# Attention rows split later in attention and earlier in the projection, kept among the sum operands; the last tile's norm first

## The chip, the core and the metric

The kernel runs on one core of one Trainium2 chip. TensorE (PE) multiplies, VectorE (DVE) and ScalarE (ACT) do the elementwise work, GpSimd (POOL) helps with copies, and SyncE (SP) issues nearly all transfers. Each engine works off its own queue in order and waits on semaphores for the others. The metric is the device time of one execution in microseconds (us); profiles are of one execution.

## The reference

One layer of a hybrid backbone over 1024 latent tokens and 256 context tokens, width 1024, all in float32. What matters here is its middle:

```
h   = modulate(rmsnorm(x, norm_mix), sh_a, sc_a)
y_m = mlstm_merge(...)                  # 4 heads of 128: columns 0..511
y_a = window_attention(...)             # 8 query heads of 64: columns 512..1023
x   = x + g_a * (concat([y_m, y_a]) @ w_out)
h   = modulate(rmsnorm(x, norm_ffn), sh_f, sc_f)
a, val = split(h @ w_up)                # 2 x 2816 columns
x   = x + g_f * ((gelu(dwconv(a)) * val) @ w_down)
out = rmsnorm(x, final_norm)
```

## The kernel before

Every large product is made of float32 operands split into a high part (a rounding copy to float32r) and a low part (the operand less its high part), and of three matmuls: high by high, high by low, low by high. So each operand costs a copy (the "hi", a cast on ACT, DVE or POOL) and a subtraction (the "lo", on DVE) before TensorE can use it.

The tokens are eight tiles of 128 rows. Attention runs as 32 pairs of heads (tile by tile, four pairs a tile) through a pipeline of stages t = 0 .. 33, written out by hand: `fill(t, slot)` puts extra work, listed in `more`, into a stage. The last two stages (t = n and n + 1, with n = 32) only drain the pipeline. The output projection's half over the mLSTM columns and its half over the attention columns of tile 0 are such extra work. `yTa` holds attention's result, transposed. `ysplit_h(b)` and `ysplit_l(b)` make the hi and lo of tile b's rows of it; the tiles `yh` and `yl` of the pool `t4` hold them.

After attention comes the attention half of the output projection, tile by tile in the order 4, 1, 5, 2, 6, 3, 7 (`order`; 7 is `last`). Each pass of this loop (L1471) works on three tiles at once: tile b in the projection, `prev` in the norm, and `pp` in the preparation of the next stage's operands.

- `wout_n(b, n)` is half n (512 columns) of tile b's projection, 12 matmuls into one of two PSUM buffers (`po`); the function that it returns (`add0`, `add1`) adds the result to the tile's rows on DVE and frees the buffer.
- `sq(b, n)` squares that half on ACT and sums it; `norm_b(b)` makes the norm (a reciprocal on DVE, a scaled copy `hn` on ACT; for the last tile in two halves, on ACT and DVE).
- `trans(b)` transposes `hn` on TensorE, and `evac(b)` copies the result out of PSUM with scale and shift, half on ACT, half on DVE, into `raws[b]`.
- `split(b, blk, w, src)` makes hi and returns the lo as a function. The results are columns of `hB`, two arrays [128, 7 blocks, 4, 512] (hi and lo): `B11`, `B21`, `B22`, and the sums `T1` to `T4`.

The up projection is a Strassen-like product: tokens 0..511 (tiles 0 to 3) and 512..1023 (tiles 4 to 7) are the two halves of one axis. So tiles 0 to 3 fill B11 and B21, each tile b >= 4 fills B22, and the pair (b, b - 4) fills T1 to T4 with sums, made by `sum1` to `sum4` on DVE. All four tiles of a half share a block: tile b has the columns (b % 4) * 128 onward, so tiles 3 and 7 have columns 384..511.

`held` is a list of lo parts and sums put off to a later place; `run(n)` does the next n of them. The order of TensorE, DVE, ACT and POOL in this region is the order of the program's text (a manual schedule, `fence`); the SP queue's order, and the place of work between the two hand-ordered regions (the split of the first up weights, `er` into `e0`), come from a planner.

After the loop stands the join: half 1 of the last tile, the norm of the last tile, its transposes, the split of the last operands, and the six products of block 0 of the up projection: a (over `e0`), then f (B22), c (T1), b (T2), e (T3), d (T4), 12 matmuls each. Their weights `R` are split there too (`wsplit_h`, with index 3, 1 and 2 for wB, wS and wA). From block 1 on the blocks repeat, and the down projection follows. The helper `sub` at L1192 records all its operations under one line.

Of the kernel before, what the change touches and what calls it, by code (L numbers as in the profile page):

```python
# [18 lines left out]
P = 128  # L19
# [59 lines left out]
def build(tc, I, out, dbg=None):  # L79
# [1111 lines left out]
    yslice = lambda b: yTa[:, :, b * P:(b + 1) * P]  # L1191
    sub = lambda e, o, x, y: e.tensor_tensor(out=o, in0=x, in1=y, op=ALU.subtract)  # L1192

    def ysplit_h(b, eng=G):
        ys[b] = [t4.tile([P, 4, P], F32R, name=f"y{n}", tag=f"y{n}", bufs=3 if n == "h" else 2) for n in "hl"]
        eng.copy(ys[b][0][:], yslice(b)) if eng is S else eng.tensor_copy(ys[b][0][:], yslice(b))

    def ysplit_l(b):
        sub(V, ys[b][1][:], yslice(b), ys[b][0][:].bitcast(F32))

    pairs = [(b, g, r) for b in range(NL) for g in range(KVH) for r in range(2)]
    pSs = [(pk, "pp")]
# [40 lines left out]
    more[n - 4, 0] += [f0.load]  # L1243
    more[n - 3, 2] += [f0.hi, f0.lo]
    tail_of(f0, n - 2)
    more[n - 5, 0] += [lambda: ysplit_h(order[0], S)]
    more[n - 5, 2] += [lambda: ysplit_l(order[0])]
    more[n - 4, 0] += [lambda: ysplit_h(order[1], S)]
    more[n - 3, 0] += [lambda: ysplit_l(order[1])]
    more[n - 2, 0] += [lambda: ysplit_h(order[2], S)]  # L1250

    attn = tc.manual_schedule(engines={mybir.EngineType.PE, mybir.EngineType.DVE, mybir.EngineType.Activation,
                                       mybir.EngineType.Pool})
# [108 lines left out]
    def load_x(b):  # L1362
        xs[b] = t3.tile([P, D], F32, name="x2", tag="x2")[:]
        nc.sync.dma_start(xs[b], x2_d[b][:])

    def wout_n(b, n, mid=None):
        ns = slice(512 * n, 512 * n + 512)
        po = pO.tile([P, 512], F32, name="po", tag="o")
        yh, yl = ys[b]
        for kt in range(4):  # L1370
            if kt == 2 and mid:
                mid()
            mm3(po[:], yh[:, kt], yl[:, kt], wos[4 + kt][0][:, ns], wos[4 + kt][1][:, ns], kt == 0, kt == 3)
        return lambda: V.tensor_tensor(out=xs[b][:, ns], in0=po[:], in1=xs[b][:, ns], op=ALU.add)

    def sq(b, n):
        if n == 0:
            hns[b] = t5.tile([P, D], F32, name="hn", tag="hn")
            rs[b] = t5.tile([P, 3], F32, name="r2", tag="r2")
        ns = slice(512 * n, 512 * n + 512)  # L1380
        S.activation(hns[b][:, ns], xs[b][:, ns], AF.Square, accum_out=rs[b][:, n:n + 1])
        if n == 1:
            run(1)
            V.tensor_scalar(out=rs[b][:, 2:3], in0=rs[b][:, 0:1], scalar1=1.0 / D, scalar2=EPS, op0=ALU.mult, op1=ALU.add)
            S.activation(rs[b][:, 0:1], rs[b][:, 1:2], AF.Sqrt, bias=rs[b][:, 2:3], scale=1.0 / D)
# [48 lines left out]
    def sum1(b):  # L1434
        sub(V, raws[b - 4][:, 0], raws[b][:, 0], raws[b - 4][:, 0])
# [35 lines left out]
    for i, b in enumerate(order):  # L1471
        prev = order[i - 1] if i else None
        pp = order[i - 2] if i > 1 else 0 if i == 1 else None
        add0 = wout_n(b, 0)
        if prev is not None:
            sq(prev, 1)
            norm_b(prev)
        run()
        if pp is not None:
            evac(pp)  # L1480
        if 0 < i and i + 2 < len(order):
            ysplit_h(order[i + 2])
        if 0 < i and i + 1 < len(order):
            ysplit_l(order[i + 1])
        if pp is not None and pp >= 4:
            held.append(split_b(pp))
        add0()
        sq(b, 0)
        if pp is not None and pp < 4:
            held.append(split(pp, B11, 2, raws[pp][:], V))  # L1490
            if late is not None:
                held.append(split_t3(late))
                held.append(split_t4(late))
            late = None
            run(1)
        if pp is not None and pp >= 4:
            sum1(pp)
            sum2(pp)
            held.append(split_t1(pp))
            held.append(split_t2(pp))  # L1500
            run(2)
            held += [lambda a=pp: sum3(a), lambda a=pp: sum4(a)]
            late = pp
        if b != last:
            add1 = wout_n(b, 1)
            trans(prev if i else 0)
            add1()
            nc.sync.dma_start(x2_d[b][:], xs[b])
        if i + 2 < len(order):
            load_x(order[i + 2])  # L1510
    ps_a, ps_a2 = (pA.tile([P, 512], F32, name="pa", tag="a") for _ in range(2))
    c3, c1 = slice(0, 384), slice(384, 512)
    add1 = wout_n(last, 1, lambda: trans(prev))
    evac(prev)
    add1()
    lo3 = split(prev, B11, 2, raws[prev][:])
    sq(last, 1)
    norm_b(last, True)
    lo3()
    prod(ps_a, e0, 0, B11, True, True, None, c3)  # L1520
    prod(ps_a2, e0, 1, B21, True, False, None, c3, range(2))
# [46 lines left out]
        return lo  # L1568


    R = load_R(0)
    sums_v(R)
    evac(last, range(4, 8))
    sub(V, R[1][:, 4], R[0][:, 1], R[1][:, 3])
    lo_b = split_b(last)
    wB = wsplit_h(R, 3)
    evac(last, range(4))
    lo_b()
    wB = wB()
    sum1(last)  # L1580
    wS = wsplit_h(R, 1)
    lo_1 = split_t1(last)
    S.copy(ar0[:], ps_a[:])
    run()
    wS = wS()
    sum2(last)
    lo_1()
    sub(V, R[1][:, 1], R[0][:, 0], R[1][:, 1])
    lo_2 = split_t2(last)
    lo_2()  # L1590
    lo_3, lo_4 = split_t3(late), split_t4(late)
    wA = wsplit_h(R, 2)
    lo_3()
    sum3(last)
    wA = wA()
    lo_5 = split_t3(last)
    lo_5()
    lo_4()
    sum4(last)
    split_t4(last)()  # L1600
    pTk.close()
    pC = pu.enter_context(tc.tile_pool(name="pC", bufs=4, space=PSUM, side="right", reuse_waits="tile"))
# [539 lines left out]
```

## Time and profile before

| | |
|---|---|
| three runs | 1279.15, 1280.69, 1274.83 us (median 1279.15) |
| profiled execution | 1275.56 us, its span 1273.7 us |
| granted TensorE clock, mean | 0.996 |
| busy, of the span | PE 97%, weight loads 83%, DVE 76%, ACT 50%, POOL 15% |
| attention's end, first matmul of tile 4's projection | 583.62 us |
| first matmul of block 1 of the up projection | 654.44 us |

A row of the profile's lists by time gives start and duration in us, the engine, the line, the operation, output <- input by the program's names, their sizes, and in brackets how long the engine stood idle before it and what it waited for. A row of the waits gives engine, output and line, what it waited for, us in total, how often, and the longest. In the rows by stretch, the pairs are busy us and instructions of PE, weight load, DVE, ACT and POOL; then follow the clock (1.00 is full), the DMA share and GB/s.

### The profile page before, as it was taken

To read this page: it belongs to the slowest core of one execution; us is meant where nothing else is said; L and a number is where in the kernel's file an instruction comes from. 1 tells how busy PE (TensorE), PEld (TensorE's weight loads), DVE (VectorE), ACT (ScalarE), POOL (GpSimd) and SP (SyncE) were. 2 spreads that over 40 slices of the span, in tenths; PEclk is the share of its full clock that TensorE was granted. 3 is DMA by queue.
4 is the path that set the end of the run, shared out by engine and by line. 5 is a ranking of instruction groups with operands and counts; after the bars stand their busy time and mean duration, and the time that the engine had idled before them with its cause. 6 is when DMAs were issued, how large, how long until landed. Compare 5 with 4: busy or idle time off the path is not lost.

```text
span 1273.7 us, 19249 instructions
## 1 busy us (share of the span) xinstructions
PE 1239.2 (97%) x7047; PEld 1062.8 (83%) x7047; DVE 972.1 (76%) x1689; ACT 639.5 (50%) x1311; POOL 187.5 (15%) x162
## 2 busy tenths in 40 slices
PE   6999999999999999999899999999999999999997
PEld 4799998999898888888788888888888888788886
DVE  4863687878787888786997877777777776867887
ACT  6732556464865777776844333333333333434435
POOL 1200000000001444221002321232231232001000
PEclk9999999999999999999999999999999999999999
DMA  9531444462355332112423322233322337975553
GB/s 357 184 125 35 142 130 144 117 177 84 84 174 160 131 111 89 62 39 102 156 74 111 120 100 92 108 108 108 108 99 91 108 117 268 344 255 179 193 197 134
DMA packets 90416, 175.64 MB, mean 138 GB/s; under 512 B 12938, under 2 KB 29522, under 8 KB 90322
## 3 DMA queue, kind: packets, MB, share of 16 engines
q1 hardware_dynamic: 90034, 173.63, 40.4%
q8 instruction: 56, 0.92, 0.3%
q10 hardware_dynamic: 288, 0.79, 0.2%
q14 instruction: 38, 0.31, 0.1%
HBM read 136.05 MB, written 38.33 MB: 137 GB/s over the span
## 4 chain that ended last, share of the span: by engine, by line
PE 81%; DVE 7%; DMA 4%; ACT 4%; issue 2%; SPq 1%; POOL 1%; ACTq 0%; DVEq 0%; POOLq 0%
PE pd L1979 14%; PE pa L1458 9%; PE pc L1458 9%; PE pp L588 7%; PE pe L1458 5%; PE pb L1458 4%; PE pd L1458 4%; PE u L1175 3%; PE pt L1152 2%; PE pv L307 2%; PE pv L309 2%; PE pv L308 2%; PE po L307 2%; PE po L308 1%; PE po L309 1%
## 5 line engine op out<-in xcount | busy, mean ns | idle before, releaser
L1563 ACT CAST wh<-Rb 128x1024 fp32r<-128x1024 f32 (+1 forms) x66 | 59.5, 904 | 143.5 <-PE pd L1458 77.1
L1979 PE MATMUL pd<-dh,al 128*128 128x512 f32 x296 | 115.4, 390 | 0.7 <-DVE al L1342 0.6
L1979 PE MATMUL pd<-dl,ah 128*128 128x512 f32 x296 | 115.2, 389 | 0.0
L1979 PE MATMUL pd<-dh,ah 128*128 128x512 f32 x296 | 115.2, 389 | 0.0
L1458 PE MATMUL pc<-hB,wh 128*128 128x512 f32 x344 | 105.6, 389 | 0.0
L1458 PE MATMUL pa<-hB,wh 128*128 128x512 f32 x336 | 103.7, 390 | 0.2 <-ACT sn L1641 0.2
L1192 DVE TENSOR_TENSOR wl<-Rb,wh 128x1024 fp32r<-128x1024 f32 (+1 forms) x66 | 68.9, 1045 | 39.2 <-ACT wh L1563 38.6
L1677 POOL TENSOR_TENSOR tt<-vt,tt 128x512 f32<-128x512 f32 x22 | 29.5, 1340 | 349.0 <-ACT tt L1671 349.0
L588 PE MATMUL pp<-hl,wh 128*128 128x512 f32 x256 | 79.4, 405 | 0.0
L307 PE MATMUL pv<-wh,hl 128*128 128x256 f32 x256 | 76.0, 297 | 0.5 <-ACT ym L601 0.5
L1458 PEld LDWEIGHTS pc<-hB,wh 128*128 128x128 f32 x344 | 64.5, 188 | 13.5
L1458 PEld LDWEIGHTS pa<-hB,wh 128*128 128x128 f32 x336 | 62.9, 188 | 14.1 <-ACT sn L1641 1.1
L309 PE MATMUL pv<-wh,hl 128*128 128x256 f32 x256 | 72.3, 283 | 0.0
L308 PE MATMUL pv<-wl,hl 128*128 128x256 f32 x256 | 72.3, 282 | 0.0
L1458 PE MATMUL pc<-hB,wl 128*128 128x512 f32 x172 | 66.4, 389 | 0.0
L1979 PEld LDWEIGHTS pd<-dh,al 128*128 128x128 f32 x296 | 55.5, 188 | 12.8 <-DVE al L1342 1.4
L1979 PEld LDWEIGHTS pd<-dl,ah 128*128 128x128 f32 x296 | 55.6, 188 | 11.9 <-DVE dl L1342 0.2
L1458 PE MATMUL pa<-hB,wl 128*128 128x512 f32 x168 | 65.4, 389 | 0.0
L1979 PEld LDWEIGHTS pd<-dh,ah 128*128 128x128 f32 x296 | 55.6, 188 | 11.6
L1159 ACT CAST ph<-pt 128x512 fp32r<-128x512 f32 (+1 forms) x88 | 46.2, 525 | 27.6 <-PE pt L1152 27.4
L1458 PE MATMUL pe<-hB,wh 128*128 128x512 f32 x176 | 54.4, 390 | 0.0
L1458 PE MATMUL pb<-hB,wh 128*128 128x512 f32 x176 | 54.2, 389 | 0.0
(1065 smaller groups left out, 3695.5 us busy)
## 6 DMA issues: line engine op xcount, KB each, us to landing
w<-in_w_ada_dram SPq DMA_DIRECT2D x64, 256.0 KB, 2.7
br<-in_w_down_dram SPq DMA_DIRECT2D x25, 512.0 KB, 5.5
Ra<-in_w_up_dram SPq DMA_DIRECT2D x22, 512.0 KB, 3.6
Rb<-in_w_up_dram SPq DMA_DIRECT2D x22, 512.0 KB, 3.5
ar<-act_s SPq DMA_DIRECT2D x44, 256.0 KB, 3.0
act_a<-tt SPq DMA_DIRECT2D x33, 256.0 KB, 2.0
act_s<-tt SPq DMA_DIRECT2D x33, 256.0 KB, 2.0
wr<-in_w_h_dram SPq DMA_DIRECT2D x16, 512.0 KB, 4.4
```

Of the source, the lines that this page charges most:

```text
L307: T.matmul(ps, st_hi, mv_hi, start=first, stop=False)
L308: T.matmul(ps, st_hi, mv_lo, start=False, stop=False)
L309: T.matmul(ps, st_lo, mv_hi, start=False, stop=last)
L588: T.matmul(pp[:, 512 * n:512 * n + 512], wkq[sw][:, kt, cs], hl[n][part][:, kt, :], start=kt == 0 and sw + part == 0, stop=kt == KT - 1 an ...
L1152: T.transpose(self.pt[i][:, (2 * kk + j) * P:(2 * kk + j + 1) * P], self.p[j][:, kb * P:(kb + 1) * P], ident[:])
L1159: S.copy(self.ph[i][:, :w], self.pt[i][:, :w])
L1175: T.matmul(self.u[:], vv[:, c, self.g], part[i][:, kk * 2 * P:(kk + 1) * 2 * P], start=kb + m == 0, stop=kb == last and m == 1)
L1192: sub = lambda e, o, x, y: e.tensor_tensor(out=o, in0=x, in1=y, op=ALU.subtract)
L1458: T.matmul(ps[:, cols], wt[sw][:, j, kt * P:kt * P + P], hB[part][:, blk, kt, cols], start=first and n == 0, stop=last and n == len(seq) - ...
L1563: S.copy(wt[0][:], src)
L1677: G.tensor_tensor(out=self.tt[:, h2_], in0=self.vt[:], in1=self.tt[:, h2_], op=ALU.mult)
L1979: T.matmul(ps[:], ac[sa][:, js], w[sw], start=first and n == 0, stop=last and n == 2, skip_group_check=not fresh)
```

## The change

Four things are done.

1. The splits of the attention rows move. Tiles 4 and 1 (the first two of the projection) were split in stages n - 5 to n - 3 and are now split in stages n and n + 1, the last two. Tile 5's hi, made in stage n - 2, and tile 2's are now made on ACT in the first pass of the loop; those of tiles 6, 3 and 7 on POOL in the second pass. The lo parts follow on DVE: tiles 5 and 2 in the first pass, 6 and 3 in the second, 7 in the third.
2. The rows of these five tiles are kept in hB, in columns 384..511 of the blocks B22 and T1 to T4, which tiles 3 and 7 fill only at the end. `yh` keeps two buffers instead of three.
3. In the loop, the hi of the B11 and B21 columns of tiles 0, 1 and 2 (1024 elements wide) moves from DVE to ACT. `split_b(pp)` comes after `add0` and the square instead of before.
4. At the end of the loop, tile 6's splits are put off: its two first sums come ahead of the last half of the projection; its B22 and T1 splits lie around the last tile's norm, which now goes ahead of the split of tile 3; T2, sum3 and sum4 go among the weight splits of block 0. The transposes of tile 3 stand one k-step later.

```diff
--- before.py
+++ after.py
@@ -1191,12 +1191,12 @@
     yslice = lambda b: yTa[:, :, b * P:(b + 1) * P]
     sub = lambda e, o, x, y: e.tensor_tensor(out=o, in0=x, in1=y, op=ALU.subtract)
 
-    def ysplit_h(b, eng=G):
-        ys[b] = [t4.tile([P, 4, P], F32R, name=f"y{n}", tag=f"y{n}", bufs=3 if n == "h" else 2) for n in "hl"]
-        eng.copy(ys[b][0][:], yslice(b)) if eng is S else eng.tensor_copy(ys[b][0][:], yslice(b))
+    def ysplit_h(b, eng=G, room=None):
+        ys[b] = room or [t4.tile([P, 4, P], F32R, name=f"y{n}", tag=f"y{n}")[:] for n in "hl"]
+        eng.copy(ys[b][0], yslice(b)) if eng is S else eng.tensor_copy(ys[b][0], yslice(b))
 
     def ysplit_l(b):
-        sub(V, ys[b][1][:], yslice(b), ys[b][0][:].bitcast(F32))
+        sub(V, ys[b][1], yslice(b), ys[b][0].bitcast(F32))
 
     pairs = [(b, g, r) for b in range(NL) for g in range(KVH) for r in range(2)]
     pSs = [(pk, "pp")]
@@ -1243,11 +1243,10 @@
     more[n - 4, 0] += [f0.load]
     more[n - 3, 2] += [f0.hi, f0.lo]
     tail_of(f0, n - 2)
-    more[n - 5, 0] += [lambda: ysplit_h(order[0], S)]
-    more[n - 5, 2] += [lambda: ysplit_l(order[0])]
-    more[n - 4, 0] += [lambda: ysplit_h(order[1], S)]
-    more[n - 3, 0] += [lambda: ysplit_l(order[1])]
-    more[n - 2, 0] += [lambda: ysplit_h(order[2], S)]
+    more[n, 0] += [lambda: ysplit_h(order[0], S)]
+    more[n, 2] += [lambda: ysplit_l(order[0])]
+    more[n + 1, 0] += [lambda: ysplit_h(order[1], S)]
+    more[n + 1, 2] += [lambda: ysplit_l(order[1])]
 
     attn = tc.manual_schedule(engines={mybir.EngineType.PE, mybir.EngineType.DVE, mybir.EngineType.Activation,
                                        mybir.EngineType.Pool})
@@ -1368,7 +1367,7 @@
         po = pO.tile([P, 512], F32, name="po", tag="o")
         yh, yl = ys[b]
         for kt in range(4):
-            if kt == 2 and mid:
+            if kt == 3 and mid:
                 mid()
             mm3(po[:], yh[:, kt], yl[:, kt], wos[4 + kt][0][:, ns], wos[4 + kt][1][:, ns], kt == 0, kt == 3)
         return lambda: V.tensor_tensor(out=xs[b][:, ns], in0=po[:], in1=xs[b][:, ns], op=ALU.add)
@@ -1478,22 +1477,25 @@
         run()
         if pp is not None:
             evac(pp)
-        if 0 < i and i + 2 < len(order):
-            ysplit_h(order[i + 2])
-        if 0 < i and i + 1 < len(order):
-            ysplit_l(order[i + 1])
-        if pp is not None and pp >= 4:
-            held.append(split_b(pp))
+        for j in ((2, 3), (4, 5, 6))[i] if i < 2 else ():
+            ysplit_h(order[j], S if j < 4 else G, [hB[n][:, B22 + j - 2, :, 3 * P:4 * P] for n in range(2)])
+        if i < 2:
+            ysplit_l(order[2 + 2 * i])
         add0()
         sq(b, 0)
+        if i < 3:
+            ysplit_l(order[(3, 5, 6)[i]])
+        if b == last:
+            break
         if pp is not None and pp < 4:
-            held.append(split(pp, B11, 2, raws[pp][:], V))
+            held.append(split(pp, B11, 2, raws[pp][:]))
             if late is not None:
                 held.append(split_t3(late))
                 held.append(split_t4(late))
             late = None
             run(1)
         if pp is not None and pp >= 4:
+            held.append(split_b(pp))
             sum1(pp)
             sum2(pp)
             held.append(split_t1(pp))
@@ -1501,21 +1503,26 @@
             run(2)
             held += [lambda a=pp: sum3(a), lambda a=pp: sum4(a)]
             late = pp
-        if b != last:
-            add1 = wout_n(b, 1)
-            trans(prev if i else 0)
-            add1()
-            nc.sync.dma_start(x2_d[b][:], xs[b])
+        add1 = wout_n(b, 1)
+        trans(prev if i else 0)
+        add1()
+        nc.sync.dma_start(x2_d[b][:], xs[b])
         if i + 2 < len(order):
             load_x(order[i + 2])
+    late = pp
     ps_a, ps_a2 = (pA.tile([P, 512], F32, name="pa", tag="a") for _ in range(2))
     c3, c1 = slice(0, 384), slice(384, 512)
+    sum1(late)
+    sum2(late)
     add1 = wout_n(last, 1, lambda: trans(prev))
     evac(prev)
     add1()
+    held.append(split_b(late))
+    sq(last, 1)
+    lo_1 = split_t1(late)
+    norm_b(last, True)
     lo3 = split(prev, B11, 2, raws[prev][:])
-    sq(last, 1)
-    norm_b(last, True)
+    lo_1()
     lo3()
     prod(ps_a, e0, 0, B11, True, True, None, c3)
     prod(ps_a2, e0, 1, B21, True, False, None, c3, range(2))
@@ -1568,35 +1575,38 @@
         return lo
 
 
+    evac(last, range(4, 8))
     R = load_R(0)
     sums_v(R)
-    evac(last, range(4, 8))
+    lo_2 = split_t2(late)
     sub(V, R[1][:, 4], R[0][:, 1], R[1][:, 3])
     lo_b = split_b(last)
     wB = wsplit_h(R, 3)
     evac(last, range(4))
     lo_b()
     wB = wB()
+    lo_2()
+    wS = wsplit_h(R, 1)
     sum1(last)
-    wS = wsplit_h(R, 1)
+    sum4(late)
+    wS = wS()
     lo_1 = split_t1(last)
-    S.copy(ar0[:], ps_a[:])
-    run()
-    wS = wS()
     sum2(last)
     lo_1()
+    sum3(late)
+    lo_2 = split_t2(last)
     sub(V, R[1][:, 1], R[0][:, 0], R[1][:, 1])
-    lo_2 = split_t2(last)
     lo_2()
     lo_3, lo_4 = split_t3(late), split_t4(late)
+    S.copy(ar0[:], ps_a[:])
     wA = wsplit_h(R, 2)
+    sum3(last)
     lo_3()
-    sum3(last)
     wA = wA()
     lo_5 = split_t3(last)
+    sum4(last)
     lo_5()
     lo_4()
-    sum4(last)
     split_t4(last)()
     pTk.close()
     pC = pu.enter_context(tc.tile_pool(name="pC", bufs=4, space=PSUM, side="right", reuse_waits="tile"))
```

## The prediction

> **What bounds the kernel now.** I read the page first, then busy times by stretch, then TensorE's waits.
>
> ```profile
> PE 1239.2 (97%) x7047; PEld 1062.8 (83%) x7047; DVE 972.1 (76%) x1689; ACT 639.5 (50%) x1311; POOL 187.5 (15%) x162
> ```
>
> TensorE is busy for 97% of the span, so a change pays or costs only where it alters TensorE's waits. The stretches (PE, weight load, DVE, ACT, POOL busy, then clock) show where those are.
>
> ```profile
> 563.80:567.30 3.50, 1.72 (x12) 1.22 (x10) 2.38 (x5) 2.91 (x7) 0.40 (x1) 0.95 0.41 162
> 567.30:574.00 6.70, 6.67 (x24) 5.79 (x25) 4.16 (x10) 3.95 (x11) 1.80 (x3) 0.52 0.00 0
> 589.09:630.04 40.95, 39.70 (x201) 32.74 (x200) 37.22 (x79) 31.13 (x73) 3.26 (x4) 1.00 0.52 179
> 630.04:640.46 10.42, 7.90 (x57) 7.54 (x56) 10.09 (x22) 7.54 (x18) 0.00 (x0) 1.00 0.14 54
> 640.46:654.44 13.98, 13.98 (x62) 11.10 (x62) 13.00 (x20) 7.32 (x12) 0.00 (x0) 1.00 0.22 77
> ```
>
> Attention ends near 583.6. The loop over the tiles 4, 1, 5, 2, 6, 3, 7 runs to about 630; the last tile's norm and the first block of the up projection end at 654.44, and the later stages are not touched. In the loop DVE is busy for 37.22 of 40.95 us and in the join for 10.09 of 10.42: DVE's queue, not TensorE's, is what can run late. TensorE's waits from 563 to 655:
>
> ```profile
> PE pt L1406 <- DVE hn L1392: 2.5, 1, 2.5
> ...
> PE po L307 <- DVE x L1374: 0.6, 1, 0.6
> ...
> PE pt L1406 <- ACT hn L1394: 0.5, 1, 0.5
> ...
> PE u L1175 <- ACT ph L1159: 0.2, 1, 0.2
> ```
>
> Loop and join together lose 3.6 us (2.5 + 0.6 + 0.5). That is all the change can win there; the row for ph lies in attention.
>
> **The change part by part.** Durations are of the profiled execution (span 1273.7 us, time 1275.56).
>
> *Rows split in the last two attention stages.* The casts of tiles 4 and 1 move behind copies that TensorE reaches late; each puts some 0.6 us ahead of one cast in ACT's queue. I take nothing for it: TensorE has output-projection matmuls to run there, and the remainders are due only at 583.6. If that cover fails it costs at most 0.6 us for each of the two. The third cast leaves a place where TensorE waited:
>
> ```profile
> 565.13 1.04 ACT L1341 CAST e0h<-er 128x1024 fp32r<-128x1024 f32 x1 [0.59 <-DMA er<-in_w_up_dram]
> ...
> 566.18 0.61 ACT L1196 CAST yh<-yTa 128x512 fp32r<-128x512 f32 x1
> ...
> 587.60 1.16 ACT L1394 ACTIVATE hn<-x,r 128x1024 f32<-128x1024 f32 x1 [0.23 <-DVE r L1389]
> ```
>
> Without the cast at 566.18 the copy behind it comes earlier, and the 0.2 us wait for ph goes: -0.2. The e0h cast ahead of it, which waits for its DMA, is not in the diff and I leave it there.
>
> *Tile 4: a new wait.* TensorE's first matmul of the second tile, and DVE's rows for the adds of the first tiles:
>
> ```profile
> 589.88 0.48 PE L307 MATMUL po<-woh,yh 128*128 128x512 f32 x1
> ```
>
> ```profile
> 587.60 0.69 DVE L1374 TENSOR_TENSOR x<-po,x 128x512 f32<-128x512 f32 x1
> 589.29 0.69 DVE L1374 TENSOR_TENSOR x<-po,x 128x512 f32<-128x512 f32 x1 [1.00 <-PE po L309]
> ...
> 593.07 0.68 DVE L1374 TENSOR_TENSOR x<-po,x 128x512 f32<-128x512 f32 x1
> ...
> 595.80 0.68 DVE L1374 TENSOR_TENSOR x<-po,x 128x512 f32<-128x512 f32 x1
> ...
> 599.54 0.68 DVE L1374 TENSOR_TENSOR x<-po,x 128x512 f32<-128x512 f32 x1
> ...
> 601.71 1.70 DVE L1192 TENSOR_TENSOR hB<-raw,hB 128x512 fp32r<-128x512 f32 x2
> 603.33 0.68 DVE L1374 TENSOR_TENSOR x<-po,x 128x512 f32<-128x512 f32 x1
> ```
>
> Tile 5's cast stands on ACT behind hn (587.60 + 1.16, its queue free 0.1 before that) and lasts 0.6; its remainder, 0.6 on DVE, now stands ahead of add0(4). So add0(4) starts near 589.9, not 587.60, and ends near 590.6; TensorE, due to reuse that PSUM buffer at 589.88, waits 0.7. One more remainder (0.6) goes ahead of add1(4): 591.1 for 589.29, and tile 4's norm chain is 1.8 late: add0(1) at 594.9.
>
> *The big split of tiles 0, 1 and 2 from DVE to ACT.* The heart of it, read from one pair of tiles on DVE and ACT:
>
> ```profile
> 607.74 0.68 DVE L1374 TENSOR_TENSOR x<-po,x 128x512 f32<-128x512 f32 x1
> 608.34 0.92 DVE L1430 CAST hB<-raw 128x1024 fp32r<-128x1024 f32 x1
> 609.29 1.23 DVE L1192 TENSOR_TENSOR hB<-raw,hB 128x1024 fp32r<-128x1024 f32 x1
> 610.43 0.69 DVE L1374 TENSOR_TENSOR x<-po,x 128x512 f32<-128x512 f32 x1
> ...
> 612.29 0.16 DVE L1389 RECIPROCAL r<-r 128x1 f32<-128x1 f32 x1
> ...
> 613.63 0.69 DVE L1192 TENSOR_TENSOR yl<-yTa,yh 128x512 fp32r<-128x512 f32 x1
> 614.23 0.69 DVE L1374 TENSOR_TENSOR x<-po,x 128x512 f32<-128x512 f32 x1
> 615.06 0.69 DVE L1192 TENSOR_TENSOR raw<-raw 128x512 f32<-128x512 f32 x1
> ...
> 617.60 0.68 DVE L1374 TENSOR_TENSOR x<-po,x 128x512 f32<-128x512 f32 x1
> ...
> 622.01 0.68 DVE L1374 TENSOR_TENSOR x<-po,x 128x512 f32<-128x512 f32 x1
> ```
>
> ```profile
> 608.44 0.63 ACT L1381 ACTIVATE hn<-x 128x512 f32<-128x512 f32 x1 [0.52 <-DVE x L1374]
> ...
> 613.54 1.48 ACT L1417 ACTIVATE raw<-pt,ada 128x128 f32<-128x128 f32 x4
> ...
> 633.08 1.04 ACT L1430 CAST hB<-raw 128x1024 fp32r<-128x1024 f32 x1 [0.46 <-DVE raw L1419]
> ```
>
> Before, DVE makes the 1024-wide cast itself. Now ACT does, behind the square that waits for add0, and DVE's next instruction is the remainder that needs it: add 0.7, square 0.64, cast 1.04, remainder 1.14, so add0 to add1 takes 3.55 us where it took 2.69 (607.74 to 610.43). DVE stands idle for 1.8 us of it, with add1 queued behind and TensorE waiting for add1 to free its PSUM buffer. The next gap, add1 to add0, loses the moved remainder (0.60, 613.63 to 614.23): 3.80 becomes 3.20. The third, add0 to add1, ran from 614.23 to 617.60 = 3.37; it holds a subtraction at 615.06 which starts when ACT's evacuation ends (613.54 + 1.48), 2.77 after the reciprocal, whatever DVE has to do before; DVE's 0.6 becomes idle time and it takes 3.97. The fourth, 617.60 to 622.01, is 4.41 less 0.60 = 3.81. A pair takes 14.53 instead of 14.27 us, though DVE has 1.9 us less to do (cast and two remainders).
>
> Carried through: add1(1) 594.9 + 3.55 = 598.4 (595.80 before); add0(5) 2.6 late less a remainder = 601.5; add1(5) 605.5 (POOL's cast no longer lengthens the pair at 601.71, 0.4); add0(2) 605.5 + 3.81 = 609.3; add0(3) 14.53 later, 623.8; add1(3) 627.4; add0(7) 630.6.
>
> ```profile
> 627.67 0.68 DVE L1374 TENSOR_TENSOR x<-po,x 128x512 f32<-128x512 f32 x1
> 629.09 0.69 DVE L1192 TENSOR_TENSOR raw<-raw 128x512 f32<-128x512 f32 x1 [0.74 <-ACT raw L1417]
> ...
> 632.91 0.68 DVE L1374 TENSOR_TENSOR x<-po,x 128x512 f32<-128x512 f32 x1
> ...
> 635.31 0.49 DVE L1392 TENSOR_SCALAR hn<-x,r 128x512 f32<-128x512 f32 x1
> 635.71 1.22 DVE L1192 TENSOR_TENSOR hB<-raw,hB 128x1024 fp32r<-128x1024 f32 x1
> ...
> 648.35 0.68 DVE L1192 TENSOR_TENSOR hB<-er,hB 128x512 fp32r<-128x512 f32 x1
> ```
>
> *The join, norm first.* Behind add0(7) stand the subtraction that waits for ACT's evacuation (632.0), a second one, and tile 3's evacuation (1.3): add1(7) at 634.65, 1.7 late. Norm first saves 0.4 (2.40 from add1 to hn at 635.31; now 2.0, the 1024-wide cast no longer being ahead of the square), so hn comes at 636.65 and TensorE's wait there shrinks from 2.5 to some 1.5 only because it arrives later itself. That cast now runs on ACT behind a 512 cast and hn, to 638.6, so tile 3's remainder starts 2.9 later than at 635.71. From there to T3's remainder of the last tile (648.35) is 12.64 us of DVE without a gap; three put-off instructions come ahead of it (the remainder of T2 and sum3 of tile 6, sum4 of the last; 0.6 each) and about 0.3 of waiting for a weight cast: 14.7. So it starts at 653.3 for 648.35. TensorE, which hardly waited there, needs it for product e; block 0 ends as long behind it as now (654.44 less 648.35): 659.4. That is **+5.0**. The two copies of hi parts that go into the sum operands' columns cost no more than in their old room; POOL's casts come earlier, hidden while DVE idles; moving the transposes by one k-step takes away part of the 0.5 wait, in the sum.
>
> Sum: +5.0 - 0.2 = +4.8 us. On the profiled execution 1275.56 + 4.8 = 1280.4. The median of the runs shown, 1279.15, is 3.6 above that execution; I expect the median of the changed kernel to stand as far above: **1284.0**. Bounds: if DVE never stood waiting for ACT, the 3.6 us of waits and the 0.2 would go, -3.8; if each of the three casts cost TensorE its whole 1.8 us of idle DVE, tile 4's 0.7 is paid and the join costs its 2.9 + 2.1 on top, +11.1. I take the value worked out, since its chain uses rows of these very instructions.
>
> **The clock.** From 563.80 TensorE was busy for 1.72 of 3.50 us, and then its clock stood at 0.52 for 6.70 us: 3.2 us lost (6.70 x 0.48), besides 1.8 of waiting. The Trainium skill, "TensorE: Matmul & The Clock Gate", Part 1, has the clock fall after an idle window of about 3.4 us, and asks for no idle gap over 3 us; the longest gap here was 1.0 us, so the trace does not agree with that as a gap. By that rule nothing in the changed stage drops the clock and the sum stays +4.8; by the row it may drop once more.
>
> **Rivals.** (1) A drop of the clock in the join, on the slower side: there TensorE will wait 1.5, 0.6 and 0.5 us within some 7 us. Against it: the stretch with the 2.5 us wait (630.04 to 640.46) kept a clock of 1.00. It decides from about half of a 3.5 us stretch idle. Price up to 3.2: +8.0, 1287.2. (2) The e0h cast slips to another place in ACT's queue, since that order is planned anew: the wait of 1.8 and the slow clock of 3.2 go, -5.0: +-0, 1279. Nothing near it changed in the diff but the cast behind it. (3) The change does what its parts suggest: ACT is ahead, the waits of 3.6 go: -3.8, 1275.4; with (2) -8.8, 1270.4. DVE's 37.22 of 40.95 speaks for it, the square between add and cast against it.
>
> **Numbers.** Forecast 0.58, (1) 0.18, (2) 0.13, (3) 0.11 (0.07 alone, 0.04 with (2)). Range 1276 to 1290: the forecast's own (1281 to 1288), (2), most of (1), and not (3). A measurement tells about 0.5%, 6.4 us, from no change. Slower: (1) and three tenths of the forecast, which reaches to 1288, 0.36; faster: (3) with (2) and part of (3), 0.08; the rest, 0.56, is within.
>
> **What would show it.** Right: DVE idle 1.3 to 1.9 us before the 1024-wide remainder three times, released by ACT's cast; TensorE's waits for x (the adds) about 3 us in total instead of 0.6; add0(4) 2.3 us later against the first output-projection matmul; a wait near 1 us before product e; from that matmul to block 1's first 75.8 us instead of 70.8. Wrong: ACT's cast done when DVE gets to it, block 0 without waits, or an add that waits for its tile's load because the up-projection weights, whose room the last remainder of the rows now frees in the third tile instead of the sixth, are queued ahead of it.

## The result, and the profile after

The change makes the kernel slightly slower: median 1280.67 us (1278.82 to 1282.55, 20 runs) against 1276.41 us (1273.73 to 1280.93, 20 runs), ratio 1.0028, 95% interval 1.0019 to 1.0037. That is +4.26 us where +4.8 was worked out, but at 1280.7 instead of 1284.0, since the level it was added to was wrong. The profiled execution took 1280.63 us (span 1278.8), 5.07 more than that of before.

TensorE's load is unchanged (first part of the page); the stretches (PE, weight load, DVE, ACT, POOL busy, clock) show where the time is:

```profile
PE 1240.6 (97%) x7047; PEld 1062.4 (83%) x7047; DVE 969.4 (76%) x1686; ACT 642.8 (50%) x1315; POOL 185.9 (15%) x161
```

```profile
564.94:568.35 3.41, 1.34 (x10) 0.99 (x9) 2.01 (x5) 2.52 (x7) 0.62 (x1) 0.98 0.62 232
568.25:571.50 3.25, 3.25 (x14) 2.95 (x15) 2.41 (x4) 1.31 (x4) 1.27 (x2) 0.50 0.00 0
...
589.61:632.95 43.34, 41.08 (x201) 32.56 (x200) 34.71 (x76) 34.24 (x76) 0.00 (x0) 1.00 0.48 170
632.95:643.85 10.90, 8.28 (x58) 7.64 (x56) 9.52 (x21) 7.81 (x19) 0.00 (x0) 1.00 0.12 48
643.85:660.16 16.31, 15.05 (x60) 10.98 (x61) 16.04 (x25) 8.55 (x13) 0.00 (x0) 1.00 0.19 66
```

The last three answer to the loop, the join and block 0, which took 40.95, 10.42 and 13.98: +2.4, +0.5 and +2.3. DVE is less busy in the loop (34.71 for 37.22) and yet later; in block 0 it now has hardly a gap (16.04 of 16.31). TensorE's waits from 563 to 661 (total, times, longest):

```profile
PE po L307 <- DVE x L1373: 2.1, 4, 0.6
PE pt L1405 <- DVE hn L1391: 1.6, 1, 1.6
PE sps L1118 <- ACT sps L1109: 1.3, 1, 1.3
PE pe L1457 <- DVE hB L1192: 0.9, 1, 0.9
PE u L1175 <- ACT p__7254 L1133: 0.8, 1, 0.8
PE pf L1457 <- ACT wh L1570: 0.6, 1, 0.6
PE pa L1457 <- DVE hB L1192: 0.4, 1, 0.4
PE pb L1457 <- DVE hB L1192: 0.4, 1, 0.4
```

The two of sps and u lie at the attention's end. The rest, with one row of 0.2 further down the list, is 6.1 us before rounding where 3.6 stood: 2.5 more, while the three stretches grew by 5.2. The list shows only half of the loss. A matmul of 512 columns is drawn 0.39 us long, though the next one normally starts 0.23 behind it, so the first 0.16 us of a stop don't show as idle, and the successor of the matmul that waited comes late too:

```profile
653.56 0.39 PE L1457 MATMUL pe<-hB,wh 128*128 128x512 f32 x1
654.81 0.50 PE L1457 MATMUL pe<-hB,wh 128*128 128x512 f32 x1 [0.86 <-DVE hB L1192]
655.15 0.39 PE L1457 MATMUL pe<-hB,wl 128*128 128x512 f32 x1
```

From start to start that is 1.25 and 0.34 us instead of twice 0.23: the listed 0.86 cost 1.13. Counted so over the same 340 intervals, TensorE lost 4.4 us before and 9.6 after, which is the 5.2. DVE's rows show the cause (start, duration, and in brackets the idle time and what ended it):

```profile
589.81 0.69 DVE L1192 TENSOR_TENSOR hB<-yTa,hB 128x512 fp32r<-128x512 f32 x1 [1.73 <-ACT hB L1196]
590.53 0.69 DVE L1373 TENSOR_TENSOR x<-po,x 128x512 f32<-128x512 f32 x1
...
595.51 0.68 DVE L1373 TENSOR_TENSOR x<-po,x 128x512 f32<-128x512 f32 x1
...
597.92 1.23 DVE L1192 TENSOR_TENSOR hB<-raw,hB 128x1024 fp32r<-128x1024 f32 x1 [1.13 <-ACT hB L1429]
599.06 0.69 DVE L1373 TENSOR_TENSOR x<-po,x 128x512 f32<-128x512 f32 x1
...
609.98 0.68 DVE L1373 TENSOR_TENSOR x<-po,x 128x512 f32<-128x512 f32 x1
612.39 1.23 DVE L1192 TENSOR_TENSOR hB<-raw,hB 128x1024 fp32r<-128x1024 f32 x1 [1.74 <-ACT hB L1429]
613.54 0.68 DVE L1373 TENSOR_TENSOR x<-po,x 128x512 f32<-128x512 f32 x1
...
624.51 0.68 DVE L1373 TENSOR_TENSOR x<-po,x 128x512 f32<-128x512 f32 x1
626.92 1.23 DVE L1192 TENSOR_TENSOR hB<-raw,hB 128x1024 fp32r<-128x1024 f32 x1 [1.73 <-ACT hB L1429]
628.06 0.68 DVE L1373 TENSOR_TENSOR x<-po,x 128x512 f32<-128x512 f32 x1
```

DVE stands still in front of each 1024-wide remainder until ACT's cast is done, with an add queued behind. Of TensorE's four listed waits for an add, one is for add0(4), behind the row remainder at 589.81 (0.64 us), two are for the adds at 613.54 and 628.06 (0.46 and 0.48), and one is for a later add, at 620.71 (0.50).

To compare executions I use three matmuls that all kernels have; these are after's:

```profile
545.11 0.40 PE L1175 MATMUL u<-pl__6945,vv 128*128 128x256 f32 x2
```

```profile
584.14 0.40 PE L307 MATMUL po<-woh,yh 128*128 128x512 f32 x1
```

```profile
660.16 0.61 PE L1457 MATMUL pa<-hB,wh 128*128 128x512 f32 x2
```

From the first to the second is the *attention's end* (39.03 us), from the second to the third the *changed stretch*: 76.02 us, before 654.44 - 583.62 = 70.82. In all 13 profiled executions (start of the first; the two stretches, in brackets how long TensorE's clock stood at 0.50; from there to the last matmul's end; then median and ratio to the kernel before, with its interval):

| kernel | first | attention's end | changed stretch | rest | median | ratio |
|---|---|---|---|---|---|---|
| before | 543.38 | 40.24 (6.8) | 70.82 | 611.81 | 1276.41 | |
| before_again | 545.53 | 38.39 | 72.10 (3.4) | 611.58 | 1276.83 | 1.0001 (0.9991–1.0011) |
| after | 545.11 | 39.03 (3.4) | 76.02 | 611.25 | 1280.67 | 1.0028 (1.0019–1.0037) |
| hi_back | 545.39 | 39.97 (6.8) | 74.57 (3.4) | 610.98 | 1278.43 | 1.0018 (1.0009–1.0026) |
| defer_lo | 544.49 | 39.40 (3.4) | 74.12 (3.4) | 611.28 | 1277.81 | 1.0007 (0.9998–1.0016) |
| join_back | 546.33 | 38.14 | 75.23 (3.4) | 611.40 | 1279.18 | 1.0025 (1.0014–1.0037) |
| three_back | 545.69 | 39.96 (6.8) | 70.44 | 612.08 | 1277.36 | 1.0011 (0.9999–1.0024) |
| before_hi | 546.80 | 38.88 (3.4) | 75.21 (3.4) | 611.34 | 1279.75 | 1.0022 (1.0012–1.0033) |
| after_e0 | 546.24 | 36.03 | 76.12 | 611.24 | 1278.22 | 1.0010 (0.9999–1.0020) |
| best | 544.85 | 35.99 | 71.90 | 611.81 | 1274.36 | 0.9981 (0.9969–0.9993) |
| before_e0 | 543.65 | 36.61 | 70.82 | 612.17 | 1274.54 | 0.9985 (0.9976–0.9994) |
| before_fill | 546.08 | 39.13 (3.4) | 70.84 | 611.60 | 1276.56 | 1.0001 (0.9991–1.0012) |
| before_both | 545.43 | 36.58 | 70.88 | 612.30 | 1273.30 | 0.9980 (0.9971–0.9989) |

Three things are read from it. First, the changed stretch is steady to 0.1 us when no half clock falls into it (70.82, 70.82, 70.84, 70.88 for four kernels with the old order), and 3.4 us at half clock cost it 1.3 (72.10). Only this pair shows that price; where I take 1.3 off another kernel's stretch below, that is an estimate. Second, code that all 13 share reaches the first of the three matmuls anywhere from 543.4 to 546.8. Third, the half clock comes in pieces of 3.4 us: in these stretches at one of two places, in join_back and after_e0 once more near the kernel's start (15.52 and 29.39), and in all 13 behind the last matmul, where no product is left to slow. Within one execution the starts lie on a grid of 3.413 us (hi_back: 568.19, 643.28 and 1274.75, which are 22 and 207 steps from the first).

### The profile page after: what moved, and what is told of

Same layout as the page of the kernel before. It is cut to its first block, busy times and chain, and to the rows that moved or that the text cites. A ratio compares the mean times of both kernels' runs of the same rounds, so it can differ in the third digit from the quotient of the medians.

```text
span 1278.8 us, 19249 instructions
## 1 busy us (share of the span) xinstructions
PE 1240.6 (97%) x7047; PEld 1062.4 (83%) x7047; DVE 969.4 (76%) x1686; ACT 642.8 (50%) x1315; POOL 185.9 (15%) x161
## 4 chain that ended last, share of the span: by engine, by line
PE 80%; DVE 7%; ACT 6%; DMA 4%; issue 3%; POOL 1%; SPq 0%; ACTq 0%; DVEq 0%; POOLq 0%
PE pd L1989 14%; PE pa L1457 9%; PE pc L1457 9%; PE pp L588 6%; PE pe L1457 5%; PE pd L1457 4%; PE pb L1457 4%; PE u L1175 3%; PE pt L1152 2%; PE pv L307 2%; PE pv L309 2%; PE pv L308 2%; PE px L309 1%; PE px L307 1%; PE px L308 1%
```

## The experiments

**hi_back.** DVE makes the 1024-wide hi halves of tiles 0, 1 and 2 again.

```diff
-            held.append(split(pp, B11, 2, raws[pp][:]))
+            held.append(split(pp, B11, 2, raws[pp][:], V))
```

> The edit puts the rounded halves (hi) of the 1024-wide splits of tiles 0, 1 and 2 back on DVE; all other parts of the change stay. Theory Q (DVE's queue, which is served in order, loses what it waits for ACT's casts): the waits of 1.13, 1.74 and 1.73 us in front of the 1024-wide remainder go, each replaced by 0.62 us of work on DVE. Worked through the queues with the rows' durations, the stretch from the first output-projection product to block 1 falls from 76.0 to about 73.7 us, and the median from 1280.7 to about 1278.4. Rival J (the loss is made in the join alone, and the loop's waits are caught up there): the stretch and the median stay within 0.5 us of the changed kernel's. Rival P (ACT was the better place for the casts): 0.5 us or more slower than the changed kernel, as DVE carries 1.9 us more.

Median 1278.43, the three waits are gone, and the stretch is 74.57, or 73.3 without the 1.3 of its half clock. Theory Q holds, 0.4 better than forecast; J and P fall. A wait for a tile's load appears here as well as in defer_lo, 1.42 us on DVE at 618.12.

**defer_lo.** The hi halves stay on ACT; only the remainder is asked for later.

```diff
             late = None
-            run(1)
```

> The edit leaves the hi casts of tiles 0, 1 and 2 on ACT, and only moves the 1024-wide remainders down DVE's queue: they are no longer asked for right behind the cast, but behind the second add of the pass, with the norm's small operations. Theory Q: it isn't ACT's cast that costs but asking for its remainder at once; the adds come 1.1 to 1.8 us earlier, DVE no longer stands still before them, and the stretch from the first output-projection product to block 1 is about 72.8 us instead of 76.0, the median about 1277.5. Rival J (join alone): no gain over 0.5 us. Rival P (DVE's queue is full, so the same work comes back as waits at the next tile's transposes): the waits for x turn into waits for hn and the gain is under 1 us.

Median 1277.81; stretch 74.12, 72.8 without its half clock, as forecast. So the cast on ACT costs little by itself; its remainder placed straight behind it in DVE's queue does the harm. One wait came in place of those removed: the up weights' loads, which the change brought forward (602.05 and 602.43; 622.11 and 622.50 in the kernel before), stand in SP's queue ahead of a tile's store; the next tile's load waits up to 6.0 us for that store (3.4 before), and an add waited for the load.

```profile
616.34 0.69 DVE L1373 TENSOR_TENSOR x<-po,x 128x512 f32<-128x512 f32 x1 [1.39 <-DMA x<-x_d]
```

**join_back.** The fourth part undone (sums of tile 6 in tile 7's pass, remainder of tile 3 ahead of the norm, the old order of block 0's operands, `kt == 2`).

```diff
-    held.append(split_b(late))
+    lo3 = split(prev, B11, 2, raws[prev][:])
     sq(last, 1)
-    lo_1 = split_t1(late)
     norm_b(last, True)
-    lo3 = split(prev, B11, 2, raws[prev][:])
-    lo_1()
     lo3()
...
```

> The edit puts the fourth part back: the last sums run inside tile 7's pass, tile 3's remainder stands ahead of the last norm, and the operands of the first up block come in the order of before; transposes of tile 3 stand behind the second contraction tile again. The split of rows and ACT's casts stay as changed. Theory Q: TensorE waits about 3.3 us for tile 7's norm instead of 1.6, but the waits of 0.4 to 1.1 us in front of the products behind it (0.41, 0.61, 0.39, 0.86) go; the stretch to block 1 falls from 76.0 to about 73.8 us, the median to about 1278.5. Rival L (the loop's waits set the time, the join is only shifted): under 0.5 us. Rival C (the longer wait for the norm lets the granted clock fall, as 3.2 us were lost at 0.52 behind the attention's end): gain gone or up to 1 us slower, with a clock under 0.8 in the slices behind the wait.

Stretch 75.23, 73.9 without its half clock, against 73.8 forecast: TensorE waits 2.5 for the norm instead of 1.6 (3.3 was forecast), and the waits of 0.4 to 0.9 behind it are gone. The median, 1279.18, gains 1.5 of the 2.2. L falls; C happened in the profiled execution and took an estimated 1.3 of the gain. The fourth part as a whole is a net loss: the norm comes earlier, but what is put off behind it comes due in block 0. Which of its steps costs how much wasn't tried apart.

**three_back.** defer_lo and join_back together, and the first add ahead of the row remainder.

```diff
-        if i < 2:
-            ysplit_l(order[2 + 2 * i])
         add0()
         sq(b, 0)
+        if i < 2:
+            ysplit_l(order[2 + 2 * i])
```

> Three edits at once on the changed kernel: the 1024-wide remainders are asked for later (as in defer_lo), the fourth part is put back (as in join_back), and in the first two passes the first add goes ahead of the row remainder, so that it no longer stands behind 1.73 us of waiting for ACT's row cast. ACT's casts and the split of rows in the first passes stay. Theory Q: the gains add up (3.2, 2.2 and 0.7 us through the queues), the stretch from the first output-projection product to block 1 falls from 76.0 to between 69.8 and 70.5 us, the level of the kernel before (70.8), and the median to 1275 to 1276.5. Rival S (the same waiting is counted twice, as DVE's and TensorE's queue end in the same join): the stretch stays above 72 us and the median above 1277.

The stretch is 70.44: the gains add up and before's level is back, with ACT's casts and the row split still as changed, but for the place of one remainder. The median of 1277.36 lies above the range given, where rival S had it, though S's stretch above 72 didn't come; what made it higher isn't shown. Its interval takes in no difference from before.

**before_hi.** The reverse: one part of the change alone, in the kernel before.

```diff
-            held.append(split(pp, B11, 2, raws[pp][:], V))
+            held.append(split(pp, B11, 2, raws[pp][:]))
```

> The kernel before with one part of the change alone: the rounded halves of the 1024-wide splits of tiles 0, 1 and 2 on ACT instead of DVE. Theory Q: DVE waits some 1.8 us for the cast three times, where it worked 0.62 us before; the adds behind come later, and the stretch from the first output-projection product to block 1 grows from 70.8 to about 73.9 us, the median from 1276.6 to about 1279.7. Rival M (the waits come only from the new mix of row remainders in the first passes): no change within 0.5 us. Rival P (DVE relieved of 1.9 us of work): 0.5 us or more faster.

```profile
597.54 1.67 DVE L1192 TENSOR_TENSOR hB<-raw,hB 128x1024 fp32r<-128x1024 f32 x1 [1.73 <-ACT hB L1430]
613.35 1.23 DVE L1192 TENSOR_TENSOR hB<-raw,hB 128x1024 fp32r<-128x1024 f32 x1 [1.73 <-ACT hB L1430]
628.47 1.23 DVE L1192 TENSOR_TENSOR hB<-raw,hB 128x1024 fp32r<-128x1024 f32 x1 [1.73 <-ACT hB L1430]
```

Median 1279.75 (1279.7 forecast), stretch 75.21, 73.9 without its half clock, as forecast; each wait is 1.73. This part alone makes the kernel 0.22% slower; M and P fall.

**before_again.** The kernel before, unchanged, for the spread of its times.

> The kernel before, unchanged, timed as often as the others, for the spread of its times. Of its first 20 times 13 lie between 1273.7 and 1277.0 and 7 between 1278.7 and 1280.9, while the 20 of the changed kernel are one group, 1278.8 to 1282.6. Theory G (clock): the upper times are executions in which TensorE's granted clock falls once more, likely behind the 2.5 us in which it waits for the last tile's norm; then their mean granted clock is lower by about 3.5/1275 = 0.0027 (0.993 beside 0.996), and the median of these runs stays at about 1276.4. Rival D (something else, such as a transfer that comes later): the mean granted clock is the same in both groups. Rival N (the groups are chance, a spread of one kind): the times fill the stretch from 1277 to 1278.7.

Over all later comparisons 102 runs of the kernel before have a recorded clock. Of the 13 with a mean of 0.994 or less, 12 took 1278.7 us or more; of the other 89, one did. So the upper times go with a lower clock, as theory G has it. Its place for the drop is not enough for them: the medians of the two groups are 1280.0 and 1276.3, 3.7 apart, while one piece in the join cost 1.3, and a mean clock of 0.994 instead of 0.996 is 2.6 us lost in 1276, where one piece of 3.4 us at half clock loses 1.7. That points to more than one piece besides the usual ones. The profiled execution was not one of them (1276.83), but it had one piece at half clock in the join, which the first profile had not; the row of the wait, the row behind it, and at the end the same place in the first profile:

```profile
632.85:636.26 3.41, 0.89 (x6) 0.57 (x5) 3.11 (x9) 2.69 (x6) 0.00 (x0) 0.99 0.00 0
```

```profile
636.25:639.50 3.25, 3.25 (x13) 3.15 (x14) 3.21 (x6) 1.10 (x4) 0.00 (x0) 0.50 0.40 161
```

```profile
636.00:639.50 3.50, 3.50 (x30) 3.47 (x29) 3.47 (x7) 1.35 (x4) 0.00 (x0) 1.00 0.38 150
```

**after_e0 and before_e0.** The first up weight's split leaves ACT and DVE for POOL. These rows of the changed kernel are what it is about (ACT, then TensorE):

```profile
567.09 1.04 ACT L1340 CAST e0h<-er 128x1024 fp32r<-128x1024 f32 x1 [0.86 <-DMA er<-in_w_up_dram]
568.04 0.16 ACT L1109 COPY sps<-sink 128x1 f32<-128x1 f32 x1
```

```profile
566.24 0.47 PE L1175 MATMUL u<-ph,vv 128*128 128x256 f32 x2 [0.76 <-ACT p__7254 L1133]
568.25 0.58 PE L1118 MATMUL sps<-kT,QT 128*128 128x256 f32 x1 [1.30 <-ACT sps L1109]
```

```diff
-    split2(e0[0][:], e0[1][:], er[:])
...
+        if i == 1:      # i == 0 in before_e0
+            G.tensor_copy(e0[0][:], er[:])
+            sub(G, e0[1][:], er[:], e0[0][:].bitcast(F32))
```

> The changed kernel with one step moved that the change left in place: the split of the first up weight (1024 wide, cast on ACT at 567.09 behind 0.86 us of waiting for its transfer, remainder on DVE at 568.17) is taken out of the attention's end and put on POOL in the second pass of the loop, where POOL is idle. Theory E (these two stand ahead of the attention's last softmax rows, and TensorE's waits of 0.76 and 1.30 us behind them also cause the slices at half clock): TensorE waits under 0.7 us there, the granted clock is 1.00 from 565 to 575 in the profiled execution, the stretch from the last attention products that all kernels share (u at 545.11) to the first output-projection product falls from 39.0 to about 37.0 us, and the median from 1280.7 to about 1278.7. Rival B (the attention's end is bound by its own chain of casts and transposes): under 0.5 us. Rival O (POOL's work slows DVE): DVE's remainders of 512 elements rise above their 0.68 us while POOL works, and the loop grows by what is gained.

> The kernel before with one step moved: the first up weight's split leaves the attention's end for POOL in the first pass of the loop. Theory E (from the changed kernel, where the same edit took 3.0 us out of the attention's end in the profiled executions and 2.45 us off the median): the attention's end falls from 38.4 to 40.2 us to about 36.0, no slice at half clock from 565 to 575, the stretch behind it stays at 70.8 (72.1 with slices at half clock in the join), the median falls from 1276.4 to about 1274. For the spread of the times: of 74 runs of the kernel before, 11 have a mean granted clock of 0.994 or less, and 10 of them are the slowest of all but one (1278.8 to 1281.6), the other 63 have 0.995 or more and a middle of 1276.4. If their extra slices at half clock come from the attention's end, none of these runs lies more than 3 us above the median, and all clocks are 0.996 or more; if from the join, one or two of 12 still do.

In both the wait for sps (1.3 us in the changed kernel, 1.0 in the kernel before) is gone and the clock is 1.00 through the attention's end. The attention's end falls to 36.03 and 36.61, and the medians to 1278.22 (-2.45) and 1274.54, with the changed stretch as it was (76.12 and 70.82). Theory E holds but for one sign: the wait for p stayed at 0.8 us in after_e0, so it wasn't this split that caused it. In before_e0 POOL did the split at 565.63, still within the attention's end, without a loss: the harm was its place in ACT's queue, ahead of copies that TensorE needs, as the rows show. (The remainder left DVE in the same edit; that part wasn't tried alone.) One of its 11 times lies 2.9 us above the median, with a clock of 0.995, so the attention's end is not the only source of the upper times.

**before_fill and before_both.** Twenty small products in TensorE's wait for tile 7's norm; before_both has the split on POOL besides.

```diff
+    for k in range(20):
+        T.matmul(ps_a[:, c1], e0[0][:, 0, 0:P], hB[0][:, B11, k % 4, 0:P], start=True, stop=True)
     trans(last, (4, 5, 6, 7))
```

> The kernel before with 20 small products (128 columns each, 0.11 us by the products of the last 128 columns) in the 2.5 us in which TensorE waits for tile 7's norm; they write columns that the next product overwrites, so that nothing is added to the result. Theory G (half-clock slices come when TensorE's busy share over some 3.4 us falls low, and in the kernel before the wait for the norm does this in part of the executions, at 1.3 us each by the two profiled ones): no slice at half clock from 634 to 645, the stretch to block 1 is 70.8 to 71.0 us, the median about 0.5 to 1 us lower, 1275.5 to 1276. Rival F (the clock doesn't depend on what TensorE does in this wait): the median stays within 0.3 us, or rises by what the products delay the transposes behind them.

> The kernel before with both edits: the first up weight's split on POOL, and the 20 small products in the wait for tile 7's norm. Theories E and G together: no slice at half clock between 565 and 645, the median 1273.3 to 1274.3, all clocks 0.997 or more, and the times spread over no more than the 3 us that arise ahead of the attention's end. Rival F: as with the split alone.

```profile
634.78 2.34 PE L1523 MATMUL pa<-hB,e0h 128*128 128x128 f32 x20
637.47 0.66 PE L1406 MATMUL pt<-ident,hn 128*128 128x128 f32 x4 [0.34 <-DVE hn L1392]
```

The products fill the wait and delay nothing (70.84, 70.88), and the clock is 1.00 there. None of the 22 times lies over 2 us above its median. But before_fill's median didn't move (1.0001), where 0.5 to 1 us was expected, which suggests that most executions lose nothing in the join. With 13 of 102 as the usual share, 22 runs without one come up by chance about one time in twenty (0.87 to the power of 22), so that the upper times arise in the join is likely, not shown. before_both has the lowest median measured, 1273.30, ratio 0.9980 (0.9971 to 0.9989); its interval overlaps those of before_e0 and best.

**best.** The changed kernel with what the runs pointed to, and the four sums of the first up weights on POOL. Of the diff only the lines for the sums are shown.

```diff
+    sums_v(R, G)
+    sums_g(R, G)
...
```

> A version that the experiments point to: the changed kernel with the 1024-wide remainders asked for later, the first add ahead of the row remainder, the first up weight's split on POOL in the second pass, the four sums of the first up block's weights on POOL too (their loads come at 603.5 and 603.9 now, 20 us before they are used), and the join's operands in the order in which TensorE takes them; tile 7's norm stays early as in the change. Theory Q: in the join DVE has 4 x 0.6 us less to do; the stretch from the first output-projection product to block 1 is about 69.2 us instead of 76.0 (70.8 before), the attention's end some 2 us shorter, and the median about 1272, 4.5 us under the kernel before. Rival O (POOL's four sums at about 1.65 us each slow DVE, or come too late for the first cast): TensorE waits over 1 us for a cast of the up weight, and the gain against the kernel before is under 2 us.

Faster than the kernel before (1274.36, ratio 0.9981) and than the changed one, but with 71.90 in the stretch instead of 69.2. POOL's sums, and DVE's rows beside them:

```profile
606.18 1.30 POOL L1545 TENSOR_TENSOR Rb<-Rb 128x512 f32<-128x512 f32 x1 [19.70 <-ACT hn L1379]
607.55 2.16 POOL L1192 TENSOR_TENSOR Rb<-Rb,Ra 128x512 f32<-128x512 f32 x1
609.79 3.31 POOL L1192 TENSOR_TENSOR Rb<-Ra,Rb 128x512 f32<-128x512 f32 x2
```

```profile
608.54 1.72 DVE L1192 TENSOR_TENSOR hB<-raw,hB 128x512 fp32r<-128x512 f32 x1
610.18 0.15 DVE L1387 RECIPROCAL r<-r 128x1 f32<-128x1 f32 x1
610.26 1.71 DVE L1192 TENSOR_TENSOR hB<-raw,hB 128x512 fp32r<-128x512 f32 x1
611.89 1.35 DVE L1417 TENSOR_SCALAR raw<-pt,ada 128x128 f32<-128x128 f32 x4
...
613.76 0.68 DVE L1192 TENSOR_TENSOR raw<-raw 128x512 f32<-128x512 f32 x1
```

Two remainders took 1.72 and 1.71 us instead of 0.68 while POOL worked, and TensorE then waited 1.31 us for the add behind them. That is rival O's cause, though its signs came out otherwise: the wait is for an add, not for a cast of the up weight, and the gain is 2.1 us where under 2 was given. POOL's sums took 2.16 us where the first took 1.30. The evacuation, which reads PSUM, kept its 1.35. The Trainium skill, "SBUF — State Buffer", section "Who interferes with whom", says that a VectorE instruction with two SBUF inputs and a GpSimd one that reads SBUF exclude each other; these rows, each slower beside the other, agree.

## Why the prediction was right or wrong

- **Bound.** Right: DVE's queue was late, and the granted clock stayed at 1.00 in the changed stretch of the profiled execution. "Loop and join together lose 3.6 us" was short, though: from start to start it is 4.4.
- **Rows in the attention's end, -0.2.** Right as far as it can be seen: the wait for ph is gone, and 38.39 became 38.14 without half clock (before_again, join_back), 40.24 became 39.97 with two pieces (before, hi_back). With one piece it can't be seen: 38.88 and 39.13 with the old rows, 39.03 and 39.40 with the new.
- **Tile 4.** Right: add0(4) comes 6.39 us behind the first output-projection product (590.53 - 584.14), where it came 3.98; 2.3 later was forecast. TensorE waited 0.64.
- **The pair of tiles.** Right to 0.05: add to add 3.55, 3.15, 3.96 and 3.81 (595.51, 599.06, 602.21, 606.17, 609.98), forecast 3.55, 3.20, 3.97 and 3.81. hi_back, defer_lo and before_hi show the cause.
- **The join.** Right: wait for the norm 1.6 (1.5), T3's remainder 69.93 us behind the first product (654.07 - 584.14; forecast 653.3 - 583.62 = 69.7), a wait of 0.86 before product e, the stretch 76.02 (75.8).
- **The sum.** +4.8 for +4.26. The stretch alone gave +5.2; the rest of the kernel gave back 0.3 to 0.6 (611.81 and 611.58 before, 611.25 after), which had no term: TensorE, which was busy for 34.76 of the 35 us from 665, now is for 35.00, since a wait of 0.2 for a copy on ACT at 698.68 is gone. The rest of it stays open.
- **The step that failed: the level.** "I expect the median of the changed kernel to stand as far above" added 3.6 us for the distance of the median from the profiled execution, read from three runs, 1274.83, 1279.15 and 1280.69. Over twenty runs that distance is 0.85 (1276.41 - 1275.56) in the kernel before and 0.04 (1280.67 - 1280.63) in the changed one. Two of the three were upper times, which are 7 of these 20 runs and 13 of 102 later ones; the medians of before in the later comparisons are 1276.2 to 1276.6. 2.7 of the error of 3.3 us is this, the other 0.5 is the sum's. Why an execution becomes an upper one is known only so far as that its clock is lower. The base to add to was the profiled execution's time, or more runs.
- **The bound of what can be told: the second step that failed.** "A measurement tells about 0.5%, 6.4 us, from no change" was read from the spread of the three, and put 0.56 of the chance on no change. Twenty runs of each gave an interval of ±0.09%, and the change shows clearly as slower, by 0.28%. The +4.8 us worked out, 0.38%, should have counted as slower, and most of the chance with it.
- **The agreement of the profiled executions** (+5.07) is partly luck: +1.73 stood before the changed code, -1.21 in the attention's end (some 0.95 of it one piece of half clock less), +5.20 in the stretch, and -0.56 behind it.
- **The clock.** I weighed the Trainium skill's rule on gaps, by which nothing would drop the clock, against the row, by which it might, and gave the drop 0.18; the row told more. "From about half of a 3.5 us stretch idle" doesn't hold as a limit either: in the kernel before, 1.52 us busy of 3.42 (631.81 to 635.23) left the clock at 1.00, and in defer_lo it fell behind 2.79 of 3.41. Among the matmuls the half clock lasts 3.4 or 6.8 us and starts at a place that moves between executions. The same section of "TensorE: Matmul & The Clock Gate", Part 1, states a window of 3.413 us that runs freely and a clock of one half; the traces agree with both, by the grid of 3.413 us and the rows at 0.50. They don't agree that it takes a long gap: in the changed kernel 1.34 of 3.41 us busy sufficed, with no gap over 1.30.
- **Rivals.** (1), the drop in the join, does occur, in five of the thirteen profiled executions, though not in that of the changed kernel; it costs 1.3 us instead of 3.2 where a pair shows it, and it occurs in the kernel before as well. (2) did not happen; with the cast moved away, in after_e0, it gave 3.0 instead of 5.0, since the changed kernel had one piece at half clock there, not two, and one wait, of 0.8, stayed. (3) fell: before_hi went the other way.

## What to carry to other kernels

Moving work to an idle engine costs when its result is the next thing in the old engine's queue: the queue stands still for the whole detour (add, square, cast) and all behind it is late. Ask for the result later, and follow the queue add by add; that replay on paper was right to 0.2 us in 76. Take the level from many runs and compare executions between matmuls that both have, for a single profiled pair differs by up to 3.4 us in code that nobody touched.

## What the runs showed of the hardware

- In these traces TensorE's clock halves for 3.4 us at a time behind stretches in which it was often idle, at places that shift from one execution to the next and lie on a grid of 3.413 us within one. A wait of 2.5 us halved it in one execution of the kernel before and not in another. Of the 1.7 us lost in a piece, 1.3 reach the end in the join (one pair), 0.5 to 1.3 in the attention's end (by the table, against 38.39 with the old rows and 38.14 with the new). What exactly it counts stays open: behind 2.79 us busy of 3.41, many of them small products, it fell too (hi_back and defer_lo), and of two stretches of the grid without a transpose, 1.97 us busy of 3.41 were followed by a drop (before_fill, from 567.16) and 1.52 were not (before, from 631.82).
- Two fp32 streams from SBUF on POOL and DVE at once (best): 1.7 us for a remainder of 0.68 on DVE, 2.16 for a sum on POOL whose neighbour took 1.30.
